# Encoder layer on one core: the look-ahead for each row's largest score takes 64 rows a product, two products side by side, and stands in twos

## The chip, the core and the metric

One core of a Trainium2 chip. The time is the device time of one execution in microseconds; the kernel before takes 1884.24 us, the median of three runs (1882.11 to 1884.48). The engines are TensorE (PE; PEld for its weight loads), VectorE (DVE), ScalarE (ACT), GpSimd (POOL) and the DMA queue of SyncE (SP).

## The reference

One layer of an encoder runs on two sequences with shared weights, "prompt" of 1,024 and "sample" of 2,048 tokens, width 1,024, in float32. Cut to what matters:

```python
h = rms_norm(x, norm_pre)
u_pool, g_pool, q, k, v, g_attn, q_x, g_x = jnp.split(jnp.einsum('btd,de->bte', h, w_in), SPLITS, axis=-1)
pool_out = multiscale_pool(u_pool, pool_w, pool_scale) * jax.nn.silu(g_pool)
# 8 query heads, 2 key/value heads, 64 wide
q = apply_rope(rms_norm(q, q_norm), cos, sin)
k = apply_rope(rms_norm(k, k_norm), cos, sin)
s = jnp.einsum('bqkgd,bskd->bkgqs', qblk, k) * 64 ** -0.5
p = jax.nn.softmax(s, axis=-1)
attn_out = jnp.einsum('bkgqs,bskd->bqkgd', p, v) * jax.nn.silu(g_attn)
# 4 heads over 256 memory tokens
x_out = memory_attention(q_x, k_m, v_m) * jax.nn.silu(g_x)
y = jnp.einsum('bte,ed->btd', jnp.concatenate([pool_out, attn_out, x_out], -1), w_out)
return x + rms_norm(y, norm_post)
```

A softmax needs a shift near the largest score of its row, so that the exponentials neither overflow nor vanish; any shift near it gives the same result.

## The kernel before, in words

**Two stages.** The first (up to some 700 us) normalises, projects and stores queries, keys, values, gates and the pool in DRAM scratch. Most products are made of three: each operand is split into a high part that the PE's fast float32 form (F32R) holds exactly and a low part, and high x high, high x low and low x high are added. The second stage, from some 700 us on, is the attention and the output, and the change lies there.

**Groups.** The second stage works on pairs of 128-token blocks, eight pairs of the sample and then four of the prompt. A pair has three groups (class `Group`): kinds 0 and 1 are the self-attention with key head 0 and 1 (256 queries x 4 heads, in two halves j of 512 columns), kind 2 the attention over the memory. A group walks its keys in chunks of 128: 16 in the sample, 8 in the prompt, 2 for the memory. One chunk of one group is a **slot**, so a sample pair has 34 slots, a prompt pair 18, and all have 344.

**Score operands.** Scores are computed transposed, keys on the partitions. KA holds the keys' high part in rows 0 to 63 and the low part in rows 64 to 127; qa holds the queries' high part twice. One product KA x qa so gives high x high plus low x high. KB holds the high part again in rows 0 to 63 and ones in row 64; qb holds the queries' low part and, in row 64, minus the largest score: the second product, of 65 rows, adds high x low and the shift.

**A slot.** The loop over the slots emits, in this order: `weights(k, 0)` (two products into one of the two PSUM buffers S, line 220, then the exponential on ACT into P, line 227); `sums` of the chunk before (P added up in z, on DVE, lines 239 and 240, half on POOL in the sample); loads; a look, if the plan has one here; things due; `weights(k, 1)`; pieces of an earlier pair's output projection (`Output.piece`, lines 359 to 361), spread over the slots between two points; things due at the half. Every fourth slot's half brings the value products of four chunks (`values`, line 252): float32 products with weights 64 columns wide, whose two j go to the two halves of the array side by side. Their slot is the first of a run of four, k%4 = 0. Order on PE, ACT, DVE and POOL is that of the program (`manual_schedule`); SP's is the scheduler's.

**Looks.** `largest` (lines 177 to 196) computes the shift ahead of the group: for 128 queries against 1,024 keys it makes two 512-wide products qa x KA into a PSUM tile N (two banks; the pool psn has two such buffers), line 191, for kind 2 four of 256 columns, line 183, and a negated maximum on DVE, line 194. So the largest is that of (high + low keys) x high queries. The last look of a group calls `shift` (line 198): the two halves' minima, a 32 x 32 transpose, and DMAs that put the row into qb's row 64. `shift` also loads KB, if this sequence's part isn't there, and the low queries. A group has 16 looks in the sample, 8 in the prompt, 2 for the memory: 344 in all, 320 of two products and 24 of four.

**The plan of looks** runs backwards over the slots, one look a slot, each for the nearest later group that starts more than LEAD = 4 slots on. 20 looks come before slot 0: they stand among the last projection's products, one after each second term (`look_ahead`). A group's loads come three slots before its first look.

**A group's end.** With n the next group's first slot: at n + 1.5 the column totals of z (`totals`, line 260, products of 32 columns) go into a tile N; at n + 2 `take` multiplies the values by the gate; at n + 2.5 `inverse` takes the reciprocal of the totals on DVE (line 272), which ends the use of that N, and sends it round through DRAM to be multiplied in (`mix_out`). A buffer of psn goes to whatever next asks while it is free; there is no fixed turn.

Of the kernel before, what the change touches and what calls it, by code (L numbers as in the profile page):

```python
# [7 lines left out]
F32 = mybir.dt.float32  # L8
F32R = mybir.dt.float32r
# [14 lines left out]
def encoder(ctx, tc, I, O):  # L24


    nc = tc.nc
# [44 lines left out]
    KA, KB, V = [], [], []  # L72

    def open_early():
        for kind in range(2):
            KA.append(early.tile([128, 2048], F32R, name=f"KA{kind}"))
            KB.append(early.tile([128, 2048], F32R, name=f"KB{kind}") if kind == 0 else None)
        KA.append(early.tile([128, 2, 2, NMEM], F32R, name="KA2"))
        KB.append(early.tile([128, 2, 2, NMEM], F32R, name="KB2"))
        for t in KB[0], KB[2]:  # L80
            nc.vector.memset(t[64:65].bitcast(F32), 1.0)

        for name in ("top",):
            lanes32[name] = [early.tile([128, 32], F32, name=f"{name}{n}") for n in range(2)]
            for t in lanes32[name]:
                nc.vector.memset(t, 0.0)
# [3 lines left out]
    def load_K(s, kind, t, hl, h):  # L90
        if (s, kind, t is KA, hl) in has_K:
            return
        has_K.add((s, kind, t is KA, hl))
        if kind == 2:
            src = DKM[hl, :, :, s].rearrange("d (c j) m -> d c j m", j=2)
            nc.sync.dma_start(out=t[2][h:h + 64].bitcast(F32), in_=src)
            return
        for a in range(0, SEQS[s][1], 1024):
            nc.sync.dma_start(out=t[kind][h:h + 64, a:a + 1024].bitcast(F32), in_=DK[s][kind][hl, :, a:a + 1024])
# [25 lines left out]
    def lanes_to_rows(t, name):  # L125

        r = early.tile([128, 32], F32, name="rows32", tag=f"r{name}", bufs=2)
        nc.vector.transpose(out=r, in_=t)
        return r
# [3 lines left out]
    class Group:  # L133
# [11 lines left out]

        def load(self):
            s, p, kind = self.s, self.p, self.kind
            for hl in range(2):
                load_K(s, kind, KA, hl, 64 * hl)
            self.qa = early.tile([128, 2, 512], F32R, name="qa", tag="qa", bufs=4)  # L150
            for h in range(2):
                self.load_q(self.qa[64 * h:64 * h + 64], 0)
            self.top = lanes32["top"][self.n % 2]
            if self.parts > 1:
                self.nb = early.tile([128, self.parts, 8], F32, name="nb", tag="nb", bufs=2)
# [20 lines left out]

        def largest(self, n):
            a, lane = self.pieces[n]
            S = psn.tile([128, 1024], F32, name="N", tag="N")
            if self.kind == 2:  # L180
                j = lane
                for x in range(4):
                    nc.tensor.matmul(S[:, 256 * x:256 * x + 256],
                                     lhsT=self.qa[:, j, 128 * x:128 * x + 128],
                                     rhs=KA[2][:, x // 2, j], start=True, stop=True)
                out, S = self.top[:, 4 * j:4 * j + 4], S.rearrange("p (x k) -> p x k", x=4)
            else:
                q = self.qa[:, lane // 4, 128 * (lane % 4):128 * (lane % 4) + 128]
                for b in range(2):
                    k = 1024 * a + 512 * b  # L190
                    nc.tensor.matmul(S[:, 512 * b:512 * b + 512], lhsT=q,  # L191
                                     rhs=KA[self.kind][:, k:k + 512], start=True, stop=True)
                out = self.nb[:, a, lane:lane + 1] if self.parts > 1 else self.top[:, lane:lane + 1]
            nc.vector.tensor_reduce(out=out, in_=S, axis=AX.X, op=ALU.max, negate=True)  # L194
            if n == len(self.pieces) - 1:
                self.shift()

        def shift(self):

            if self.parts > 1:  # L200
                nc.vector.tensor_tensor(out=self.top[:, 0:8], in0=self.nb[:, 0], in1=self.nb[:, 1],
                                        op=ALU.min)
            self.qb = early.tile([128, 2, 512], F32R, name="qb", tag="qb", bufs=3)
            load_K(self.s, self.kind, KB, 0, 0)
            self.load_q(self.qb[0:64], 1)
            r = lanes_to_rows(self.top, "top")
            row = self.qb[64:65].rearrange("o j (l b r) -> o (j l) b r", b=4, r=32)
            for b in range(4):
                nc.sync.dma_start(out=row[:, :, b].bitcast(F32), in_=r[32 * b:32 * b + 8])


        def weights(self, k, j):
            if j == 0:
                self.P[k] = dbl.tile([128, 2, 512], F32, name="P", tag="P", bufs=6)
            S = pss.tile([128, 512], F32, name="S", tag="S")
            keys = slice(128 * k, 128 * k + 128)
            for n, (K, q) in enumerate(((KA, self.qa[:, j]), (KB, self.qb[0:65, j]))):
                rows_ = slice(0, 128 if n == 0 else 65)
                if self.kind < 2:
                    nc.tensor.matmul(S, lhsT=K[self.kind][rows_, keys], rhs=q, start=n == 0, stop=n == 1)  # L220
                    continue
# [178 lines left out]
    LEAD, RUN = 4, 4  # L400
    pairs = [Pair(s, p) for s in (1, 0) for p in range(SEQS[s][1] // 256)]
    groups = []
# [5 lines left out]
    slots = [(g, k) for g in groups for k in range(g.chunks)]  # L408
# [3 lines left out]
    def at(slot, f, *args):  # L412

        later.setdefault(slot, []).append((f, args))

    def due(slot):
        for f, args in later.pop(slot, ()):
            f(*args)  # L418

    first = {}  # L420
# [18 lines left out]
    for g in groups:  # L439
        n, c = first[g], g.chunks  # L440
# [11 lines left out]

    looks, n = {}, len(slots)
    left = {g: list(range(len(g.pieces))) for g in groups}
    while any(left.values()):
        n -= 1
        able = [g for g in groups if left[g] and first[g] - LEAD > n]
        if able:  # L460
            looks[n] = (able[0], left[able[0]].pop())
    ahead = [looks[n] for n in sorted(looks) if n < 0]
    loads = {}
    for n, (g, k) in looks.items():
        if k == 0:
            loads.setdefault(max(n - 3, -1), []).append(g)

    order = {mybir.EngineType.PE, mybir.EngineType.Activation, mybir.EngineType.DVE,
             mybir.EngineType.Pool}

    def look_ahead():

        if ahead:
            g, n = ahead.pop(0)
            g.largest(n)


    with ExitStack() as p1:
# [345 lines left out]
        early = psn = None  # L824
        for sb, (kind, s, nb, b0) in enumerate(SB):
            groups = groups_of(sb)
            nxt = []
            for gi, (src, pieces, run) in enumerate(groups):
# [7 lines left out]
                if last and gi == 3:  # L836
                    front.close()
                    early = ctx.enter_context(tc.tile_pool(name="early", bufs=1, side="right", reuse_waits="tile"))
# [22 lines left out]
    own = pool("p2one", 1)  # L861
# [4 lines left out]

    ones = own.tile([128, 32], F32, name="ones")
    nc.vector.memset(ones, 1.0)
    KB[1] = own.tile([128, 2048], F32R, name="KB1")
    nc.vector.memset(KB[1][64:65].bitcast(F32), 1.0)  # L870
    V += [own.tile([128, 16, 64], F32, name=f"V{kind}") for kind in range(2)]
    V.append(own.tile([128, 2, 4, 64], F32, name="V2"))
    wo_hi = own.tile([128, NC, D], F32R, name="wo_hi")
# [3 lines left out]
    with tc.manual_schedule(engines=order):  # L877
        slot = 0
        while slot < len(slots) or later or fill:
            g, k = slots[slot] if slot < len(slots) else (None, 0)  # L880
            if g:
                g.weights(k, 0)
            if 0 < slot <= len(slots):
                h, kh = slots[slot - 1]
                h.sums(kh)
            for x in loads.get(slot, ()):
                x.load()
            if slot in looks:
                looks[slot][0].largest(looks[slot][1])
            due(slot)  # L890
            if g:
                g.weights(k, 1)
            pauses = sum(x is None for x in fill)
            n = -(-(len(fill) - pauses) // max(1, until[0] - slot - pauses)) if fill else 0
            for _ in range(n):
                x = fill.pop(0)
                if x is None:
                    break
                out, h, c, start, final = x
                out.piece(h, c, start, final)  # L900
                if final:
                    if h == 0 and not out.last:

                        for n in sorted(later):
                            for x in [x for x in later[n] if x[0].__name__ in ("square", "norm", "out")]:
                                later[n].remove(x)
                                x[0](*x[1])
                    at(slot + END, out.half_out, h)
                    at(slot + 1 + END, out.square, h)
                    if h == 1:  # L910
                        at(slot + 2, out.norm)
                        at(slot + 3, out.out)
            due(slot + END)
            slot += 1

# [41 lines left out]
```

## Time and profile before

| | |
|---|---|
| median of three runs | 1884.24 us |
| span of the profiled execution | 1878.7 us |
| first S product, last slot's first product | 699.1 us, 1836.6 us |
| eight sample pairs, three prompt pairs | 850.6 us, 216.8 us |
| mean granted clock of TensorE | 0.994 |

The three runs are all the times there are; the profiled execution's own is its span, first to last instruction, and the median lies 5.6 us above it.

How to read the lines: "L191 PE MATMUL N<-KA,qa 128*128 128x512 f32 x640 | 207.5, 405 | 17.9 <-..." is a group: line, engine, operation, tiles written and read, weight and data shape, count; busy us of the group as a union, mean ns of one; idle time of the engine before them and what ended it. PE's records overlap, since a product begins while the last is still leaving the array: what a product costs is the distance to the next one's start. A time line has start, length, engine and the same names, and merges neighbours of one kind ("x16"); a value product in float32 leaves two records, so four chunks make 16. A window has its length, then for PE, PEld, DVE, ACT and POOL the busy time and count, then the granted clock, the DMA share and GB/s.

### The profile page before, as it was taken

The numbers are of one execution on the slowest core, as the hardware profiler recorded it, in microseconds if no ns is written. First come the engines' busy times: TensorE is split into PE (matmuls) and PEld (weight loads), VectorE is DVE, ScalarE is ACT, GpSimd is POOL, SyncE is SP. The second block draws the span as 40 slices with busy tenths as digits, with TensorE's granted clock in tenths as the row PEclk, the third lists the DMA queues.
The fourth block names the chain that finished last, engine by engine and source line by source line (L and its number), as shares of the span: only waits on it lengthen the run. The fifth ranks groups of instructions, "written<-read, shape, count | busy, mean of one in ns | idle before, by whom it ended". The sixth has DMA issues, their size and how long they took to land. (4 is left out here: it accounts for less than half of the span.)

```text
span 1878.7 us, 23531 instructions
## 1 busy us (share of the span) xinstructions
PE 1813.4 (97%) x8520; PEld 1279.4 (68%) x8520; DVE 1135.6 (60%) x1312; ACT 696.8 (37%) x1266; POOL 846.5 (45%) x748
## 2 busy tenths in 40 slices
PE   7999999999999999999999999999999999999997
PEld 6888888988988884465564656556465655565564
DVE  7745145431544168867768576776858576757744
ACT  5523234222422115444435344443434343333331
POOL 3655016520446007845638374563837452413311
PEclk9999999999999999999999999999999999999998
DMA  7634454254434926212122221212222153223211
GB/s 244 201 113 120 108 162 132 73 154 116 121 99 114 216 65 173 73 27 79 48 79 62 68 62 29 80 45 79 63 68 63 51 137 78 96 85 96 87 43 62
DMA packets 148485, 181.83 MB, mean 97 GB/s; under 512 B 21504, under 2 KB 118416, under 8 KB 148368
## 3 DMA queue, kind: packets, MB, share of 16 engines
q1 hardware_dynamic: 148368, 180.33, 33.9%
q8 instruction: 67, 1.10, 0.3%
q14 instruction: 50, 0.41, 0.1%
HBM read 126.50 MB, written 53.62 MB: 96 GB/s over the span
## 5 line engine op out<-in xcount | busy, mean ns | idle before, releaser
L227 ACT ACTIVATE P<-S 128x512 f32<-128x512 f32 x688 | 399.3, 598 | 555.5 <-PE S L220 430.8
L194 DVE TENSOR_REDUCE nb<-N 128x1 f32<-128x1024 f32 x256 | 311.7, 1218 | 239.8 <-PE N L191 239.0
L239 POOL TENSOR_TENSOR z<-z,P 128x512 f32<-128x512 f32 x224 | 318.4, 1421 | 222.5 <-ACT P L227 217.4
L252 PE MATMUL acc<-P,V 128*64 128x512 f32 (+1 forms) x1472 | 319.4, 576 | 0.5
L220 PE MATMUL S<-qa,KA 128*128 128x512 f32 x640 | 274.6, 429 | 9.7 <-ACT P L227 9.7
L63 POOL TENSOR_TENSOR rs<-rs,mhalf 128x1 f32<-128x1 f32 (+2 forms) x100 | 101.0, 1013 | 401.8 <-DVE rs L61 401.8
L240 DVE TENSOR_TENSOR z<-z,P 128x512 f32<-128x512 f32 (+1 forms) x272 | 271.0, 996 | 13.1 <-ACT P L227 12.9
L220 PE MATMUL S<-qb,KB 65*128 65x512 f32 x640 | 254.0, 397 | 0.0
L550 PE MATMUL pz<-hT_hi,w_hi 128*128 128x512 f32 x592 | 233.1, 394 | 1.3 <-ACT vmst L808 0.8
L552 PE MATMUL pz<-hT_hi,w_lo 128*128 128x512 f32 x592 | 232.1, 392 | 0.5 <-DVE w_lo L69 0.5
L551 PE MATMUL pz<-hT_lo,w_hi 128*128 128x512 f32 x592 | 232.3, 392 | 0.0
L191 PE MATMUL N<-KA,qa 128*128 128x512 f32 x640 | 207.5, 405 | 17.9 <-DVE rz L272 11.2
L252 PEld LDWEIGHTS acc<-P,V 128*64 128x64 f32 x1472 | 98.3, 138 | 178.7 <-issue 169.6
L220 PEld LDWEIGHTS S<-qa,KA 128*128 128x128 f32 x640 | 120.4, 188 | 143.9 <-issue 72.6
L194 DVE TENSOR_REDUCE top<-N 128x1 f32<-128x1024 f32 (+1 forms) x88 | 107.0, 1219 | 94.3 <-PE N L191 74.5
L191 PEld LDWEIGHTS N<-KA,qa 128*128 128x128 f32 x640 | 116.6, 191 | 60.9 <-DVE nb L194 21.9
L550 PE MATMUL pz<-w_hi,hT_hi 128*128 128x384 f32 (+1 forms) x416 | 140.2, 338 | 0.9 <-ACT hT_hi L68 0.8
L551 PE MATMUL pz<-w_lo,hT_hi 128*128 128x384 f32 (+1 forms) x416 | 139.4, 335 | 0.8 <-DVE w_lo L69 0.8
L552 PE MATMUL pz<-w_hi,hT_lo 128*128 128x384 f32 (+1 forms) x416 | 139.7, 338 | 0.0
L359 PE MATMUL py<-wo_hi,mix 128*128 128x512 f32 x352 | 137.7, 391 | 0.0
L360 PE MATMUL py<-wo_lo,mix 128*128 128x512 f32 x352 | 137.7, 391 | 0.0
L361 PE MATMUL py<-wo_hi,mix 128*128 128x512 f32 x352 | 137.4, 390 | 0.0
(120 smaller groups left out, 2479.5 us busy)
## 6 DMA issues: line engine op xcount, KB each, us to landing
wraw<-w_in SPq DMA_DIRECT2D x15, 1536.0 KB
dg<-gst SPq DMA_DIRECT2D x48, 256.0 KB
qa<-dq SPq DMA_DIRECT2D x48, 256.0 KB
gz<-rows SPq DMA_DIRECT2D x72, 128.0 KB
x<-x_sample SPq DMA_DIRECT2D x16, 512.0 KB
xr<-x_sample SPq DMA_DIRECT2D x16, 512.0 KB
y_sample<-xr SPq DMA_DIRECT2D x16, 512.0 KB
dq<-qst SPq DMA_DIRECT2D x96, 64.0 KB
```

The costliest lines, as they stand in the source:

```text
L191: nc.tensor.matmul(S[:, 512 * b:512 * b + 512], lhsT=q, rhs=KA[self.kind][:, k:k + 512], start=True, stop=True)
L194: nc.vector.tensor_reduce(out=out, in_=S, axis=AX.X, op=ALU.max, negate=True)
L220: nc.tensor.matmul(S, lhsT=K[self.kind][rows_, keys], rhs=q, start=n == 0, stop=n == 1)
L227: nc.scalar.activation(out=self.P[k][:, j], in_=S, func=AF.Exp)
L239: nc.gpsimd.tensor_tensor(out=z[:, :cut], in0=a[:, :cut], in1=P[:, :cut], op=ALU.add)
L240: nc.vector.tensor_tensor(out=z[:, cut:], in0=a[:, cut:], in1=P[:, cut:], op=ALU.add)
L252: nc.tensor.matmul(self.acc[64 * j:64 * j + 64, x], lhsT=v, rhs=P[:, j, x], start=(k, i) == (0, 0), stop=k == self.chunks - 1, skip_group_ ...
L359: nc.tensor.matmul(ps, lhsT=mh, rhs=wo_hi[:, c, cols], start=first, stop=False)
L360: nc.tensor.matmul(ps, lhsT=mh, rhs=wo_lo[:, c, cols], start=False, stop=False)
L550: nc.tensor.matmul(ps, lhsT=sh, rhs=mh, start=c == 0, stop=False)
L551: nc.tensor.matmul(ps, lhsT=sh, rhs=ml, start=False, stop=False)
L552: nc.tensor.matmul(ps, lhsT=sl, rhs=mh, start=False, stop=c == n - 1)
```

## The change

- The looks take KA and KB in halves: KA's rows 64 to 127 now hold the keys' high part and its rows 0 to 63 the low part (for the scores nothing changes, since qa holds the high queries twice), and KB's rows 0 to 63 hold the high part as before. Each product of a look takes 64 rows: the one over rows 0 to 63 reads KB, the one over rows 64 to 127 KA. They write different banks. For kind 2 the four products go in the order 0, 2, 1, 3, so that neighbours take different halves and banks.
- A look is so high x high alone; the low part of the keys no longer enters the largest score.
- The plan gives two looks to slots with k%4 = 0 and k%4 = 2, none to the others (before slot 0 one each, as before). In slots with k%4 = 2 they stand where the look stood, ahead of `weights(k, 1)`; in slots with k%4 = 0 they stand behind the output pieces, right before the value products. A group's last look so comes 6 slots ahead of it instead of 5.
- KB is loaded with KA, ahead of the first look, instead of in `shift`; KB1 moves from the second stage's pool to the one that is opened early, with its memset.

```diff
@@ def open_early
-            KB.append(early.tile([128, 2048], F32R, name=f"KB{kind}") if kind == 0 else None)
+            KB.append(early.tile([128, 2048], F32R, name=f"KB{kind}"))
...
-        for t in KB[0], KB[2]:
+        for t in KB:
             nc.vector.memset(t[64:65].bitcast(F32), 1.0)
@@ Group.load
+            load_K(s, kind, KB, 0, 0)
             for hl in range(2):
-                load_K(s, kind, KA, hl, 64 * hl)
+                load_K(s, kind, KA, hl, 64 - 64 * hl)
@@ Group.largest
+            halves = (slice(0, 64), KB), (slice(64, 128), KA)
             S = psn.tile([128, 1024], F32, name="N", tag="N")
             if self.kind == 2:
                 j = lane
-                for x in range(4):
+                for x in (0, 2, 1, 3):
+                    rows_, K = halves[x // 2]
                     nc.tensor.matmul(S[:, 256 * x:256 * x + 256],
-                                     lhsT=self.qa[:, j, 128 * x:128 * x + 128],
-                                     rhs=KA[2][:, x // 2, j], start=True, stop=True)
+                                     lhsT=self.qa[rows_, j, 128 * x:128 * x + 128],
+                                     rhs=K[2][rows_, x // 2, j], start=True, stop=True)
...
                 for b in range(2):
                     k = 1024 * a + 512 * b
-                    nc.tensor.matmul(S[:, 512 * b:512 * b + 512], lhsT=q,
-                                     rhs=KA[self.kind][:, k:k + 512], start=True, stop=True)
+                    rows_, K = halves[b]
+                    nc.tensor.matmul(S[:, 512 * b:512 * b + 512], lhsT=q[rows_],
+                                     rhs=K[self.kind][rows_, k:k + 512], start=True, stop=True)
@@ Group.shift
-            load_K(self.s, self.kind, KB, 0, 0)
@@ the plan of looks
+    def room(n):
+        return 1 if n < 0 else (2, 0, 2, 0)[slots[n][1] % 4]
...
-        able = [g for g in groups if left[g] and first[g] - LEAD > n]
-        if able:
-            looks[n] = (able[0], left[able[0]].pop())
+        for _ in range(room(n)):
+            able = [g for g in groups if left[g] and first[g] - LEAD > n]
+            if able:
+                looks.setdefault(n, []).insert(0, (able[0], left[able[0]].pop()))
...
+    def look(slot):
+        for g, n in looks.pop(slot, ()):
+            g.largest(n)
@@ the loop over the slots
-            if slot in looks:
-                looks[slot][0].largest(looks[slot][1])
+            if k % 4:
+                look(slot)
             due(slot)
...
+            look(slot)
             due(slot + END)
```

More of the change, by code (lines that the diff above doesn't have):

```diff
@@ L458, in encoder @@
         n -= 1
-        able = [g for g in groups if left[g] and first[g] - LEAD > n]
-        if able:
-            looks[n] = (able[0], left[able[0]].pop())
-    ahead = [looks[n] for n in sorted(looks) if n < 0]
+        for _ in range(room(n)):
+            able = [g for g in groups if left[g] and first[g] - LEAD > n]
+            if able:
+                looks.setdefault(n, []).insert(0, (able[0], left[able[0]].pop()))
+    ahead = [x for n in sorted(looks) if n < 0 for x in looks[n]]
     loads = {}
-    for n, (g, k) in looks.items():
-        if k == 0:
-            loads.setdefault(max(n - 3, -1), []).append(g)
+    for n in looks:
+        for g, k in looks[n]:
+            if k == 0:
+                loads.setdefault(max(n - 3, -1), []).append(g)
     order = {mybir.EngineType.PE, mybir.EngineType.Activation, mybir.EngineType.DVE,
              mybir.EngineType.Pool}
+    def look(slot):
+        for g, n in looks.pop(slot, ()):
+            g.largest(n)
     def look_ahead():
@@ L868, in encoder @@
     nc.vector.memset(ones, 1.0)
-    KB[1] = own.tile([128, 2048], F32R, name="KB1")
-    nc.vector.memset(KB[1][64:65].bitcast(F32), 1.0)
     V += [own.tile([128, 16, 64], F32, name=f"V{kind}") for kind in range(2)]
```

## The prediction

> **What bounds the kernel now.** I read the page's head first.
>
> ```profile
> span 1878.7 us, 23531 instructions
> ...
> PE 1813.4 (97%) x8520; PEld 1279.4 (68%) x8520; DVE 1135.6 (60%) x1312; ACT 696.8 (37%) x1266; POOL 846.5 (45%) x748
> ```
>
> TensorE looks like the bound, and the change halves one of its groups. But busy PE time is a union of overlapping, modelled durations, so the next views are the time line of PE, for what a product costs and where PE waits, and the window view of one pair, which puts prices on stages. The first of these groups is the exponential, the other three belong to a look:
>
> ```profile
> L227 ACT ACTIVATE P<-S 128x512 f32<-128x512 f32 x688 | 399.3, 598 | 555.5 <-PE S L220 430.8 <-issue 72.9 <-POOL o L290 25.0
> ...
> L194 DVE TENSOR_REDUCE nb<-N 128x1 f32<-128x1024 f32 x256 | 311.7, 1218 | 239.8 <-PE N L191 239.0
> ...
> L191 PE MATMUL N<-KA,qa 128*128 128x512 f32 x640 | 207.5, 405 | 17.9 <-DVE rz L272 11.2 <-DVE nb L194 5.7
> ...
> L183 PE MATMUL N<-KA,qa 128*128 128x256 f32 x96 | 16.0, 288 | 2.1 <-DVE top L194 2.1
> ```
>
> A look is two 512-wide products (320 of them) or four 256-wide ones (24), then a maximum of 1.22 us on DVE. The time line gives the step of a product and the price of changing the array's shape:
>
> ```profile
> 999.44 0.39 PE L220 MATMUL S<-qb,KB 65*128 65x512 f32 x1
> 999.76 3.65 PE L252 MATMUL acc<-P,V 128*64 128x512 f32 x16
> 1003.34 0.50 PE L220 MATMUL S<-qa,KA 128*128 128x512 f32 x1
> 1003.68 0.39 PE L220 MATMUL S<-qb,KB 65*128 65x512 f32 x1
> 1003.91 0.63 PE L191 MATMUL N<-KA,qa 128*128 128x512 f32 x2
> 1004.38 0.39 PE L220 MATMUL S<-qa,KA 128*128 128x512 f32 x1
> ```
>
> A full product follows the last after 0.23 us, a look takes 0.47 (1003.91 to 1004.38). Into the value products (64 columns each, two at a time) the step is 0.32, so entering costs 0.09; the eight pairs at 0.43 account for 3.43 of the 3.58 us up to 1003.34, the other 0.15 being a late second pair and the way out; the next full product also comes after 0.34 instead of 0.23. In all a stay in the other shape costs about 0.14 on the way in and 0.20 on the way out, 0.34 us.
>
> The rows on which the argument turns come next: two slots without a look and without output pieces, and two with one look each.
>
> ```profile
> 1790.00 0.41 PE L220 MATMUL S<-qa,KA 128*128 128x512 f32 x1
> ...
> 1790.85 0.50 PE L220 MATMUL S<-qa,KA 128*128 128x512 f32 x1 [0.21 <-ACT P L227]
> 1791.19 0.39 PE L220 MATMUL S<-qb,KB 65*128 65x512 f32 x1
> 1791.42 0.42 PE L220 MATMUL S<-qa,KA 128*128 128x512 f32 x1
> ...
> 1792.84 0.36 PE L224 MATMUL S<-qa,KA 128*128 128x256 f32 x1
> ```
> ```profile
> 1790.20 1.08 ACT L227 ACTIVATE P<-S 128x512 f32<-128x512 f32 x2 [0.34 <-PE S L220]
> 1791.62 1.14 ACT L227 ACTIVATE P<-S 128x512 f32<-128x512 f32 x2 [0.34 <-PE S L220]
> ```
> ```profile
> 1546.81 0.42 PE L220 MATMUL S<-qa,KA 128*128 128x512 f32 x1
> ...
> 1547.30 0.63 PE L191 MATMUL N<-KA,qa 128*128 128x512 f32 x2
> ...
> 1548.22 0.48 PE L220 MATMUL S<-qa,KA 128*128 128x512 f32 x1
> ```
>
> Without a look a slot lasts 1.42 us (1790.00 to 1791.42, 1791.42 to 1792.84), with one 1.41. Two S buffers make a ring: products 0.34 and 0.23, 0.04 to the exponential, 0.55 to 0.60 for it, 0.05 back. The ring, not PE, sets a slot that has no pieces, and one look stands in its gap for nothing. About half of the slots are of this kind.
>
> **The change, part by part.** *Products.* Of the 344 looks (320 + 24) 20 come before slot 0 and 324 in slots; counted through the plan's loop, these make 87 twos beside the value products (k%4 = 0) and 75 in the third slot (k%4 = 2). If two half-height products run side by side, as the two half-width ones above do, a look takes 0.235: 324 x 0.235 = 76 us less PE work. That is gross, and here is what stands against it.
>
> *Shape changes.* No row shows a 64-row product. The nearest is the value products' stay, 0.34 us in and out. Bounds for a third-slot two: 0 (the array need not empty for a change of rows) to twice the 0.34, since a weight load of 128 columns would stand open there. Beside the values only one more change is added, so half of each. I take 0.34 and 0.14: the one change of shape in the trace always costs. 75 x 0.34 + 87 x 0.14 = 38 us. The Trainium skill (TensorEngine Tiling, Key Properties) has the rule against this change: a new tiling mode, though not a new tile in the same mode, drains TensorE. By that rule the 38 stay and the sum is 1921; without it they go, and it is the first rival's 1881. That page counts row tiling among the modes; here only column tiling shows it. The skill also has four-row packing at 3.07 times instead of four (TensorE: Matmul & The Clock Gate, Measured speedup vs the span model); an estimate from that share, 0.31 a look for 0.235, would add up to 23 us gross.
>
> *Stages.* One sample pair, cut at its runs of four slots (fifth: the memory group's two):
>
> ```profile
> 1117.42:1128.54 11.12, 10.74 (x50) 5.34 (x49) 8.50 (x10) 4.68 (x8) 9.56 (x8) 1.00 0.39 102
> 1128.54:1138.95 10.41, 9.81 (x42) 5.07 (x40) 8.41 (x9) 4.83 (x9) 6.01 (x5) 1.00 0.17 52
> 1138.95:1154.00 15.05, 15.05 (x70) 10.21 (x70) 10.20 (x13) 5.54 (x10) 9.07 (x7) 1.00 0.00 0
> 1154.00:1168.82 14.82, 14.82 (x66) 9.87 (x64) 7.48 (x10) 5.81 (x11) 3.88 (x3) 1.00 0.01 2
> 1168.82:1178.95 10.13, 10.13 (x58) 5.93 (x57) 5.57 (x8) 3.38 (x7) 1.84 (x2) 1.00 0.41 103
> 1178.95:1192.49 13.54, 13.09 (x71) 8.94 (x68) 10.08 (x11) 5.88 (x11) 7.88 (x5) 1.00 0.61 175
> 1192.49:1206.01 13.52, 13.52 (x60) 8.78 (x59) 8.72 (x10) 4.68 (x8) 4.46 (x4) 1.00 0.07 23
> 1206.01:1216.59 10.58, 10.04 (x42) 5.16 (x42) 8.04 (x10) 6.39 (x13) 9.08 (x7) 1.00 0.09 25
> 1216.59:1226.59 10.00, 9.93 (x42) 5.21 (x42) 9.93 (x11) 4.53 (x8) 9.92 (x7) 1.00 0.29 103
> sum 109.17, PE 107.12 PEld 64.51 DVE 76.93 ACT 45.72 POOL 61.71; mean PE 11.90 PEld 7.17 DVE 8.55 ACT 5.08 POOL 6.86
> ```
>
> *A run without pieces* (second, eighth, ninth), walked in the new order with the ring's numbers, 0 being its second slot's first product. That slot takes 1.43. In the third, the first S product ends at 2.0, the two looks run from 2.09 to 2.61, the second S product starts at 2.70. The fourth starts at 3.27, but its second product waits for the exponential of 2.70's S until 4.13. The next first slot starts at 4.70, its second product again waits, until 5.56; looks 6.22 to 6.74, values 6.88 to 10.31, and the run ends at 10.4. Measured before: 10.41, 10.58, 10.00. So nothing is gained: second and fourth slot lose a look that was free, third and first get two that are not. I take 0, +0.2 and +0.4 (one of 10.58's slots also holds pieces).
>
> *A run with pieces* is PE's own (13.52 of 13.52): 4 x 0.235 less, 0.34 and 0.14 more, -0.46. Fourth and seventh run: -0.5 each; third, whose first slot has no pieces, and fifth: 0.
>
> *A group's end* gets worse. Its total takes one of the two N buffers in the second slot and gives it back at the reciprocal, which DVE has behind the third slot's maxima. Before:
>
> ```profile
> 1236.65 0.73 PE L191 MATMUL N<-KA,qa 128*128 128x512 f32 x2 [0.31 <-DVE nb L194]
> ...
> 1238.91 0.50 PE L191 MATMUL N<-KA,qa 128*128 128x512 f32 x1 [0.59 <-DVE rz L272]
> ```
> ```profile
> 1235.37 1.23 DVE L194 TENSOR_REDUCE nb<-N 128x1 f32<-128x1024 f32 x1
> 1236.51 0.68 DVE L266 TENSOR_TENSOR o<-acc,gate 128x512 f32<-128x512 f32 x1
> 1237.11 1.75 DVE L272 RECIPROCAL rz<-N 128x256 f32<-128x256 f32 x1
> ```
>
> The look at 1236.65 waits for the maximum before it (1235.37 + 1.23), since the total holds the other buffer. With two looks in that slot the second can only take the first one's buffer: after its product (0.4) and its maximum (1.22) it starts 1.7 us after the first instead of 0.24, about 1.45 us of PE at 31 of the 36 group ends (after the other five no look is left), and the S product, ACT and all of PE queue behind it. What before paid there (as above) goes. Walked like the run above, the first run, 11.12, becomes 12.4 (+1.3); the sixth holds two ends, 13.54 becomes 15.8 (+2.3).
>
> A pair: 1.3 + 0 + 0 - 0.5 + 0 + 2.3 - 0.5 + 0.2 + 0.4 = +3.2, eight pairs +26.
>
> *Sequence of 1,024.* The stage of the first three pairs:
>
> ```profile
> 1549.70:1766.48 216.78, 206.74 (x962) 130.34 (x961) 147.62 (x144) 80.03 (x153) 59.79 (x34) 0.99 0.30 87
> ```
>
> 72.3 a pair, with three group ends in 18 slots and pieces in few of them: the same terms give +3.5 for the ends, -0.5 and -0.3 for pieces and rest, +2.7; three pairs and the few looks of the last, +9.
>
> *The rest.* The 20 early looks stand alone among full products: 0.235 + 0.34 for 0.47, +2 us. KB's loads (256 KB each, six for kinds 0 and 1) move on SP's queue from after a group's looks to ahead of its KA and queries; they are issued three slots (over 4 us) before the first look, or some 30 us before it in the projections, so I put them at 0, and at a transfer of some 2 us for each of three later kinds if that cover fails. KB1's memset goes from one side of the stage to the other: 0. DVE's maxima are as many and as long. The loss of the low part changes only the shift.
>
> Sum: 26 + 9 + 2 = +37 us on the profiled execution's 1878.7, so 1916; the median of the runs lies 5.6 over that span (1884.24 - 1878.67), which gives 1921.
>
> **Rivals.** *Rows change shape free.* Then the 38 and the 2 fall away and the sum is -3: 1881. For it: only column shapes are seen to cost. It shows in the step from the last S product to a look, 0.23 instead of 0.32.
>
> *The second look at a group's end finds a buffer.* -31 x 1.2 = -37: 1884. Against it is the row at 1236.65.
>
> *PE's saving comes out whole* (faster): PE is the bound in every slot, so 76 less and 40 more count in full, -36: 1848. It decides if slots without a look fall below 1.42 us; the slots at 1790 speak against it, 97% PE for it.
>
> *The halves run one after the other.* A look stays at 0.47 and the changes of shape are added: some 60 of the 76 us come back (the rest is in the ring's gaps): 1981. Against it the value products, two records to each step.
>
> **How the numbers follow.** Forecast 0.60, free rows 0.14, buffer found 0.06, whole saving 0.10, halves in turn 0.10. A measurement of this kernel tells apart 0.2%, 4 us. Slower: all of halves in turn, 0.58 of the forecast, 0.06 of the two rivals near zero: 0.74. Same: 0.08 from these. Faster: whole saving and the rest, 0.18. Range 1870 to 1962: the upper end is the forecast with the shape changes at twice their price (+38) and a little over, the lower one the free rows with a wait of 1.1 instead of 1.45 us at the 31 ends (-11); left out are the last two rivals, 0.2.
>
> **What would show it.** Right: look products of one pair start within 0.02 us; the step into a two is about 0.32 and the S product after it 0.09 late; slots without pieces or look stay at 1.4; in 31 places the second look starts 1.5 us or more after the first, released by DVE; PE waits on ACT grow, DVE busy time is unchanged. Wrong: if the first and the sixth run of the pair above do not grow, or if runs without pieces fall below 9.7 us.

## The result, and the profile after

The changed kernel takes 1986.71 us (median of 4 runs, 1985.69 to 1989.26) where the kernel before takes 1883.17 (4 runs, 1878.91 to 1884.48): ratio 1.0557, 95% interval 1.0541 to 1.0572. It is slower, as forecast, but by 104 us instead of 37, and 25 us above the upper end of the range. In the profiled executions the span grows by 107 us, from 1878.7 to 1985.8.

The head of the changed kernel's page, the lines that answer to those shown of before:

```profile
span 1985.8 us, 23531 instructions
...
PE 1868.0 (94%) x8520; PEld 1224.0 (62%) x8520; DVE 1219.5 (61%) x1312; ACT 684.0 (34%) x1266; POOL 836.3 (42%) x748
...
PEclk9999999999999988999998999989998999899999
```

PE is busy for 55 us longer although its looks were halved, and the clock row has eights in the second stage, which begins in the fifteenth slice. Before, that row had only nines up to its last slice:

```profile
PEclk9999999999999999999999999999999999999998
```

The slices round, so the trace's clock records were added up: TensorE spends 155.1 us at half of its clock (23 stretches, the last at the very end of the trace) where it spent 25.4 before (5 stretches). The cores view agrees: a mean clock of 0.961 over 1985.8 us is 2 x 0.039 x 1985.8 = 155 us at a half.

The windows of the two stages (length; busy time and count of PE, PEld, DVE, ACT, POOL; clock; DMA share; GB/s), the sample's eight pairs and the prompt's three, first before (the sample alone; the prompt's row stands in the prediction), then after:

```profile
699.11:1549.70 850.59, 828.38 (x3701) 493.52 (x3700) 610.43 (x638) 368.28 (x668) 497.51 (x341) 1.00 0.26 72
```
```profile
700.70:1633.40 932.70, 868.60 (x3702) 450.96 (x3700) 683.42 (x636) 356.51 (x668) 493.76 (x342) 0.94 0.23 65
1633.40:1871.90 238.50, 216.97 (x962) 122.78 (x961) 156.48 (x143) 78.55 (x153) 55.05 (x34) 0.94 0.27 78
```

So of the 107 us the sample has 82.1 (forecast 26), the prompt's three pairs 21.7 (9), what comes before slot 0 has 1.6 (2), and the rest 1.7. PE's busy time in the sample grows by 40 us, but the stage by 82: the other 42 are waits.

The same pair as in the prediction, cut at the same slots:

```profile
1162.25:1175.88 13.63, 11.62 (x50) 4.98 (x49) 11.65 (x11) 4.64 (x8) 8.06 (x7) 0.93 0.25 58
1175.88:1188.28 12.40, 11.90 (x42) 4.92 (x41) 8.29 (x9) 4.70 (x9) 7.11 (x5) 0.80 0.14 44
1188.28:1203.41 15.13, 14.85 (x69) 9.25 (x69) 11.82 (x12) 5.36 (x10) 8.00 (x6) 1.00 0.00 0
1203.41:1218.36 14.95, 14.69 (x66) 8.77 (x64) 8.69 (x10) 5.65 (x12) 4.29 (x4) 1.00 0.01 2
1218.36:1228.26 9.90, 9.90 (x56) 5.53 (x56) 6.39 (x8) 3.10 (x7) 5.02 (x4) 1.00 0.37 98
1228.26:1245.82 17.56, 14.69 (x71) 9.31 (x68) 11.83 (x11) 5.65 (x11) 4.73 (x4) 0.90 0.44 140
1245.82:1259.39 13.57, 13.33 (x59) 7.73 (x57) 7.71 (x8) 4.50 (x9) 3.86 (x3) 1.00 0.07 21
1259.39:1269.85 10.46, 9.70 (x40) 4.29 (x41) 9.95 (x9) 6.12 (x13) 8.92 (x7) 1.00 0.09 26
1269.85:1280.83 10.98, 10.13 (x42) 4.26 (x41) 10.70 (x11) 4.47 (x8) 10.82 (x8) 1.00 0.34 121
sum 118.58, PE 110.80 PEld 59.03 DVE 87.04 ACT 44.19 POOL 60.81; mean PE 12.31 PEld 6.56 DVE 9.67 ACT 4.91 POOL 6.76
```

The three runs of four that grew most, the first, the second and the sixth, are the three with a clock below 1.00. They are where a group ends, and right behind. The time line of PE there (start, length; in brackets the idle time before it and what ended it):

```profile
1170.83 0.50 PE L195 MATMUL N<-KB,qa 64*128 64x512 f32 x1
1170.83 0.50 PE L195 MATMUL N<-KA,qa 64*128 64x512 f32 x1
...
1172.98 0.49 PE L195 MATMUL N<-KB,qa 64*128 64x512 f32 x1 [1.65 <-DVE nb L198]
1172.98 0.49 PE L195 MATMUL N<-KA,qa 64*128 64x512 f32 x1
1173.40 0.50 PE L223 MATMUL S<-qa,KA 128*128 128x512 f32 x1
1173.74 0.43 PE L223 MATMUL S<-qb,KB 65*128 65x512 f32 x1
1173.98 0.62 PE L223 MATMUL S<-qa,KA 128*128 128x512 f32 x1
1174.39 0.63 PE L223 MATMUL S<-qb,KB 65*128 65x512 f32 x1
1174.86 0.79 PE L223 MATMUL S<-qa,KA 128*128 128x512 f32 x1
1175.45 0.63 PE L223 MATMUL S<-qb,KB 65*128 65x512 f32 x1
...
1179.06 4.49 PE L255 MATMUL acc<-P,V 128*64 128x512 f32 x16
```

The wait of the forecast is there: the second look starts 2.15 us after the first, released by DVE's maximum. What the forecast did not have comes behind it. From 1173.98 on the S products last 0.62 to 0.79 us instead of 0.39 to 0.50, and follow each other at 0.41 to 0.59 instead of 0.23 and 0.34. The value products at 1179.06 take 4.49 us; before they took 3.65. That is the half clock, and here it lasts 6.8 us.

Setting the clock records beside all 31 group ends with two looks shows how regular this is. PE waits 1.65 to 1.67 us at ten of them, and behind each of the ten the clock falls. At fifteen it waits 1.32 or 1.33 us, and the clock falls behind three. The remaining six waits, from 1.45 to 3.65 us, have four falls in or behind them. That makes 17 of the stage's 22 falls; the other five, of 3.4 us each, stand elsewhere and have no wait of this kind.

Beside values and in third slots the halves do run side by side. The time line of PE in a third slot:

```profile
1185.30 0.39 PE L223 MATMUL S<-qb,KB 65*128 65x512 f32 x1
1185.62 0.49 PE L195 MATMUL N<-KB,qa 64*128 64x512 f32 x1
1185.63 0.49 PE L195 MATMUL N<-KA,qa 64*128 64x512 f32 x1
1185.96 0.39 PE L195 MATMUL N<-KB,qa 64*128 64x512 f32 x1
1185.96 0.39 PE L195 MATMUL N<-KA,qa 64*128 64x512 f32 x1
1186.28 0.50 PE L223 MATMUL S<-qa,KA 128*128 128x512 f32 x1
1186.62 0.40 PE L223 MATMUL S<-qb,KB 65*128 65x512 f32 x1
```

The two products of a look start within 0.01 us. The way in takes 0.32 instead of 0.23 (1185.30 to 1185.62), the first pair 0.34, the second, with the way out, 0.32, and the next full product 0.34 more. Six steps of full products would be 1.38 us from 1185.30 to 1186.62; it is 1.32.

### The profile page after: what moved, and what is told of

Same layout as the page of the kernel before. It is cut to its first block, busy times and chain, and to the rows that moved or that the text cites. A ratio compares the mean times of both kernels' runs of the same rounds, so it can differ in the third digit from the quotient of the medians.

```text
span 1985.8 us, 23531 instructions
## 1 busy us (share of the span) xinstructions
PE 1868.0 (94%) x8520; PEld 1224.0 (62%) x8520; DVE 1219.5 (61%) x1312; ACT 684.0 (34%) x1266; POOL 836.3 (42%) x748
## 5 line engine op out<-in xcount | busy, mean ns | idle before, releaser
L230 ACT ACTIVATE P<-S 128x512 f32<-128x512 f32 x688 | 387.1, 598 | 673.5 <-PE S L223 445.5
L243 DVE TENSOR_TENSOR z<-z,P 128x512 f32<-128x512 f32 (+1 forms) x272 | 326.7, 1201 | 146.6 <-ACT P L230 140.7
L198 DVE TENSOR_REDUCE nb<-N 128x1 f32<-128x1024 f32 x256 | 303.3, 1216 | 122.5 <-PE N L195 122.2
L255 PE MATMUL acc<-P,V 128*64 128x512 f32 (+1 forms) x1472 | 341.3, 609 | 0.0
L223 PE MATMUL S<-qa,KA 128*128 128x512 f32 x640 | 305.7, 478 | 34.9 <-ACT P L230 34.7
L223 PE MATMUL S<-qb,KB 65*128 65x512 f32 x640 | 267.4, 418 | 0.0
L223 PEld LDWEIGHTS S<-qa,KA 128*128 128x128 f32 x640 | 126.1, 197 | 222.4 <-ACT P L230 121.7
L255 PEld LDWEIGHTS acc<-P,V 128*64 128x64 f32 x1472 | 103.5, 146 | 197.7 <-issue 190.7
L195 PE MATMUL N<-KB,qa 64*128 64x512 f32 x320 | 137.6, 487 | 44.0 <-DVE nb L198 35.6
L195 PE MATMUL N<-KA,qa 64*128 64x512 f32 x320 | 137.6, 487 | 0.0
```

Source lines behind the costliest of these rows:

```text
L195: nc.tensor.matmul(S[:, 512 * b:512 * b + 512], lhsT=q[rows_], rhs=K[self.kind][rows_, k:k + 512], start=True, stop=True)
L230: nc.scalar.activation(out=self.P[k][:, j], in_=S, func=AF.Exp)
L243: nc.vector.tensor_tensor(out=z[:, cut:], in0=a[:, cut:], in1=P[:, cut:], op=ALU.add)
L255: nc.tensor.matmul(self.acc[64 * j:64 * j + 64, x], lhsT=v, rhs=P[:, j, x], start=(k, i) == (0, 0), stop=k == self.chunks - 1, skip_group_ ...
```

## The experiments

The theory after the result: the group ends' wait, by itself priced nearly right, makes the clock fall to a half, and the slow products behind it are most of what is missing. The rivals: the half-height products cost more than 0.34 a stay; twos of any height cost it, by the ring and the waits; the moved loads cost something. In each diff below the lines stand against the changed kernel, unless another is named; "..." marks what is left out. "Half-clock time" is added up from the clock records of the profiled execution.

**Work in the wait.** Six spare full-height products at each group's end, between the two looks. They go into the S buffer that the next S product overwrites, so the result stays as it is:

```diff
+        here = looks.pop(slot, ())
+        for i, (g, n) in enumerate(here):
+            if i and slot in ends:
+                keep_busy(slots[slot][0], 6)
+            g.largest(n)
```

> The changed kernel with six dummy full-height products between the two looks at each of the 31 group ends (into an S buffer that the next S product overwrites; results unchanged). Theory, clock: 155 us of the changed kernel's profile run at half the clock (25 before), set off by PE standing idle while the second look waits; of its +107 us of span about 65 are that lost clock. Then added work makes it faster: low-clock time under 70 us, time about 1945 us (1930 to 1960). Rival, waits alone: where the clock is low PE waits for others anyway, so it costs nothing; 1987 us within 5, or slower.

Measured: 1942.93 us, ratio 1.0319 (1.0295 to 1.0343). Added work makes the changed kernel 44 us faster. Its page:

```profile
span 1940.1 us, 23903 instructions
...
PEclk9999999999999999999999999999999999999998
```

The half-clock time falls from 155.1 to 18.8 us. ACT's hold on S, on the other hand, stays as it was in the changed kernel; the view of waits (us in all, times, longest), first after, then with the spare products:

```profile
PEld S L223 <- ACT P L230: 121.7, 225, 1.7
```
```profile
PEld S L232 <- ACT P L239: 123.0, 226, 1.7
```

So it is the clock and not the ring that the added work mends. Its half-clock time is no more than that of the kernel before (25.4 us).

**Work where PE is idle for other reasons.** Two spare products in odd slots in which no piece is pending:

```diff
+            if g and k % 2 and not fill:
+                keep_busy(g, 2)
             if k % 4:
                 look(slot)
```

> The changed kernel with two dummy full-height products in every slot with odd k that holds no output pieces, where a look of the kernel before stood (results unchanged). If the exp ring sets these slots, the products cost nothing there. Theory, clock, in the form that a stretch of about 3.4 us with PE working under half of it halves the next one: more work in the look-free slots shortens the low stretches but does not take away the idle time that sets them off: low-clock time 155 to about 90 to 120 us, time 1960 to 1975 us. Rival, waits alone: 1987 us or up to 15 slower.

Measured: 1983.84 us, 1.0540 (1.0514 to 1.0567), half-clock time 127.8, outside the 90 to 120 and the 1960 to 1975 us that were expected, and at the rival's 1987 within 5. But the edit did much less than its expectation says. Its condition asks for an empty list of pieces, and from the second sample pair on that list also holds the pauses between pieces. The view of the spare products' line (count, duration in ns, first and last start) shows where they stand:

```profile
L139 PE MATMUL S<-qa,KA x42: 390/397/796, 705.7 to 827.3; 128*128 128x512 f32 x42
```

So there are 42 of them, in 21 slots: the 17 odd slots of the first sample pair and four of the second. From slot 0 to slot 34 the half-clock time fell from 27.3 to 6.8 us and the pair from 105.7 to 100.3 us; the pairs from the third on have no spare product. This run so does not say what such work is worth behind the waits of the other pairs, nor whether it is free in the ring's gap. As far as it goes, it agrees with the clock theory.

**Seven products of half height in the wait**, which need no change of shape against the looks beside them. Here the lines stand against the first experiment's kernel:

```diff
-                             lhsT=KA[g.kind][:, 0:128] ..., rhs=g.qa[:, 0], ...)
+                             lhsT=KB[g.kind][0:64, 0:128] ..., rhs=g.qa[0:64, 0], ...)
-                keep_busy(slots[slot][0], 6)
+                keep_busy(slots[slot][0], 7)
```

> As the run with the six dummies at the group ends, but with seven of half height in the looks' own shape, one after the other. They add the same busy time and no change of shape. If the clock follows the time in which PE works, whatever the height: low-clock time under 40 us and 31 times 0.34 us less than that run, about 1932 us. If it follows how much of the array works: low-clock time near 100 us, 1955 to 1975 us.

Measured: 1940.19 us, 1.0302 (1.0272 to 1.0333), half-clock time 34.2; the time lies 8 us above what was expected, the half-clock time inside it. Products that use half of the array hold the clock up about as well as full ones, so the clock goes by the time in which PE works rather than by the share of the array that does. This pair, whole, has no half clock in it and so shows what the change costs without:

```profile
1146.86:1160.01 13.15, 12.53 (x56) 5.79 (x56) 11.17 (x11) 4.55 (x8) 8.07 (x6) 1.00 0.26 60
...
1185.66:1200.64 14.98, 14.72 (x66) 8.78 (x64) 8.70 (x10) 5.66 (x12) 4.30 (x4) 1.00 0.00 0
...
1210.54:1226.57 16.03, 15.81 (x85) 10.61 (x81) 10.42 (x9) 5.55 (x11) 4.24 (x4) 1.00 0.48 145
1226.57:1240.14 13.57, 13.33 (x60) 7.72 (x58) 9.14 (x10) 4.52 (x9) 4.68 (x4) 1.00 0.13 33
...
1250.61:1261.58 10.97, 10.13 (x41) 4.26 (x41) 10.69 (x11) 4.48 (x8) 10.81 (x8) 1.00 0.33 121
...
1146.86:1261.58 114.72, 110.81 (x502) 60.47 (x502) 86.78 (x83) 43.99 (x84) 61.46 (x44) 1.00 0.20 58
```

These are the first, fourth, sixth, seventh and ninth run and the whole pair: 114.72 us, where before has 109.17 and the change 118.58.

**One look at a group's end, the other in the next slot:**

```diff
+    ends = {first[g] + g.chunks + 2 for g in groups}
...
+        if n in ends or n - 1 in ends:
+            return 1
         return 1 if n < 0 else (2, 0, 2, 0)[slots[n][1] % 4]
```

> The changed kernel's plan with one look instead of two in the slot where a group's total holds an N buffer, and one in the slot after it. Both theories say that the wait of about 1.5 us at 31 ends goes, some 40 us; the clock theory adds most of 65 us of lost clock: 1885 to 1905 us, low-clock time under 50 us. Waits alone: 1945 us.

Measured: 1929.65 us, 1.0244 (1.0223 to 1.0265), half-clock time 55.4; a pair without half clock takes 111.90 us. It is the best of the versions that keep the twos elsewhere, but 25 us above what was expected at most, and the half-clock time is over 50: the ends do not carry all that is left. Of that pair's 2.7 us over the kernel before, 1.3 lie in the second run (11.74 for 10.41) and 1.0 in the ninth (10.97 for 10.00).

**Only the height, only the twos, only the loads.** One look a slot as before, but of two half-height products:

```diff
-        return 1 if n < 0 else (2, 0, 2, 0)[slots[n][1] % 4]
+        return 1 if n < 0 else 1
...
-            if k % 4:
-                look(slot)
+            look(slot)
```

> Half-height products side by side, but one look a slot where the look stood before: the product form without the twos. By the terms of the forecast each look saves 0.235 us and pays 0.34 us for two changes of shape, +34 us if PE set every slot, some +20 with the gaps of the exp ring; no wait at group ends is added. So 1900 to 1915 us and low-clock time under 60 us. Rival (shape changes free): 1870 us or less.

Measured: 1913.61 us, 1.0156 (1.0134 to 1.0178), half-clock time 46.1, as expected. Run seven, which is PE's own, goes from 13.52 to 14.14:

```profile
1210.46:1224.60 14.14, 14.14 (x59) 7.82 (x58) 9.66 (x10) 4.67 (x8) 4.11 (x5) 1.00 0.08 22
```

Each of its four slots takes 0.15 to 0.17 us more: a stay costs 0.235 + 0.155 = 0.39, and one look saves only 0.235.

The twos of the plan, but each look over all 128 rows of KA:

```diff
-                for x in (0, 2, 1, 3):
-                    rows_, K = halves[x // 2]
+                for x in range(4):
+                    rows_, K = slice(0, 128), KA
...
-                    rows_, K = halves[b]
+                    rows_, K = slice(0, 128), KA
```

> The twos alone: the changed plan with the full-height products of before (no change of shape, nothing side by side). If the twos (waits at group ends, look-free slots bound by the exp ring) are the cost and the half-height products a gain in PE time: without lost clock some 36 us above the changed kernel's 1922 (1987 less 65 of clock), and with the array working longer per slot less clock lost than 65, so 1960 to 1990 us and low-clock time 60 to 120 us. Rival, the changes of shape are the main cost: 1925 us or less.

Measured: 1983.68 us, 1.0534 (1.0501 to 1.0566), half-clock time 98.1. This too is as expected: the twos alone cost as much as the whole change, and on top of them half height changes the total by nothing. By slots it does gain: in the seventh run of the pair shown, the slot with the values takes 6.66 us instead of 6.92 and the third 3.16 instead of 3.21. But the changed kernel has 57 us more at half clock, 155.1 against 98.1; that this is what eats the gain was not tried.

Both edits together, so that nothing is left but the moved loads and buffers:

> Only the change's moved loads and buffers (KB with KA, the high part in KA's rows 64 to 127, KB1 in the early pool), with the products and the plan of before. Every theory has these at nothing: 1884 us within 4. If it is over 1890, part of the +103 is theirs.

Measured: 1882.02 us, 1.0002 (0.9989 to 1.0016). The loads cost nothing.

**Both halves on rows 0 to 63**, where two products cannot run at one time:

```diff
-            halves = (slice(0, 64), KB), (slice(64, 128), KA)
+            halves = (slice(0, 64), KB), (slice(0, 64), KB)
```

> The changed kernel with both halves of a look on rows 0 to 63, so that they cannot run side by side (same values). If they do run side by side in the changed kernel, 344 times 0.235 us come on top, of which some 60 us show outside the ring's gaps, less some clock, since the array works longer: 2005 to 2040 us. If they did not gain from it: 1987 us within 5.

Measured: 2083.77 us, 1.1063 (1.1030 to 1.1095). Running side by side is worth 97 us to the changed kernel, more than the 18 to 53 expected, and the half-clock time was to shrink and grew, to 222.6 us. The prediction's gross saving of 76 us and 67 us more at half clock, at the first experiment's rate of 44 us for 136, would make 76 + 22 = 98; but why the clock falls more often here was not settled.

**The sums behind the looks.** DVE's addition of z stands ahead of the maxima. In slots with a two in third place it is emitted behind them:

```diff
+            two = k % 4 == 2 and slot in looks
-            if 0 < slot <= len(slots):
+            if 0 < slot <= len(slots) and not two:
...
             if k % 4:
                 look(slot)
+            if two:
+                slots[slot - 1][0].sums(slots[slot - 1][1])
```

> The changed kernel, only that in the slots with k%4 = 2 which hold two looks the column sums z of the chunk before (half on DVE, half on POOL in the sample) are emitted behind the two looks instead of ahead of them, so that both maxima stand before the addition on DVE. If DVE's addition, which takes 1.4 us there and stands ahead of the first maximum, is what made the second look at a group's end start 2.15 us after the first instead of the 1.7 us of the forecast, it now starts 1.65 to 1.75 us after it, 31 x 0.45 = 14 us come back, and a part of the half-clock time with them (155 us now): 1945 to 1975 us. If DVE's place in the order is not the cause (the first look itself is late, or the maxima run one after the other anyway and only they count), the step stays above 2 us and the time at 1980 to 1990. If the later sums hold the P buffers and so ACT, the waits of ACT on DVE and POOL grow and it is slower than 1990.

Measured: 1976.36 us, 1.0500 (1.0476 to 1.0524), half-clock time 122.9. DVE's place in the order is a cause, but a small one. The end shown above now has the second look 1.82 us behind the first; the time lines of PE and of DVE:

```profile
1167.21 0.50 PE L195 MATMUL N<-KA,qa 64*128 64x512 f32 x1
...
1169.03 0.49 PE L195 MATMUL N<-KB,qa 64*128 64x512 f32 x1 [1.32 <-DVE nb L198]
```
```profile
1167.75 1.23 DVE L198 TENSOR_REDUCE nb<-N 128x1 f32<-128x1024 f32 x1 [1.78 <-PE N L195]
```

Counted over the 31 ends, only ten had 2.15 to 2.17 in the changed kernel, and fifteen had 1.82 or 1.83 already; one, behind an addition of 2.37 us, had 4.15. The mean goes from 2.03 to 1.83, 6 us in all and not the 14 expected. The 32 us less at half clock would by the first experiment's rate (44 us for 136) be worth 10 by themselves, so the two do not add up cleanly. Nor does the length of a wait alone decide on the clock: here PE waits 1.32 or 1.33 us at every end, and the clock falls behind 13 of the 31, where in the changed kernel it fell behind 3 of 15 such waits.

**A better plan.** One full-height look a slot as before, and half-height twos only beside values where the next slot has pieces, so that both look places are really PE's. The form of a look and its place in the loop follow from the set `twos`. First at three places of a sample pair and one of a prompt pair:

```diff
+    twos = {first[pair.groups[0]] + r for pair in pairs[1:] for r in ((12, 16, 22) if pair.s else (8,))}
...
-        return 1 if n < 0 else (2, 0, 2, 0)[slots[n][1] % 4]
+        return 2 if n in twos else 0 if n - 1 in twos else 1
```

> One full-height look a slot as before, but beside the value products whose next slot holds output pieces (three places in each sample pair after the first, one in each prompt pair) two half-height looks side by side, and none in that next slot. In the changed kernel these places alone gained: the slot of the value products grew by 0.21 to 0.23 us, the next one fell by 0.45 to 0.47. So 25 places times 0.25 us, 6 us: 1877 us against 1883, ratio 0.9966, low-clock time as before (under 35 us). If half-height looks lose wherever they stand: 1885 us or more.

Measured: 1885.44 us, 1.0012 (1.0001 to 1.0023); a gain was expected. The fourth and the seventh run gained, 14.82 to 14.62 and 13.52 to 13.22, but the memory group's run rose from 10.13 to 10.25 and the prompt's places, which the plan had taken for PE's own, by 1 to 5 us each. The same plan at full height:

> The same plan with full-height looks throughout: it moves a look of 0.47 us from one slot that PE sets to another, so 1883 us within 3. If the plan and not the form brings the gain: 1877 us too.

Measured: 1887.89 us, 1.0032 (1.0023 to 1.0042), slower than expected: the plan by itself costs some 6 us. At the same places half height is then worth 2.4 us. With the two places that gained, and no others (against the first of these two kernels):

```diff
-    twos = {first[pair.groups[0]] + r for pair in pairs[1:] for r in ((12, 16, 22) if pair.s else (8,))}
+    twos = {first[pair.groups[0]] + r for pair in pairs[1:] for r in ((12, 22) if pair.s else ())}
```

> The plan of the run before it, cut to the places whose runs fell there: the fourth and the seventh run of each sample pair (13.52 to 13.22 and 14.83 to 14.62 us in that trace), without the memory group's place (10.13 to 10.25) and the prompt's (12.96 to 14.07). Seven or eight pairs times 0.5 us: -4 us, 1878 against 1882, ratio 0.998. If the time stays at 1882, what the runs gained is given back elsewhere.

Measured: 1878.96 us, 0.9981 (0.9970 to 0.9993), the only version that beats the kernel before, and by 3.4 us. Its fourth and seventh run, both PE's own for their whole length:

```profile
1153.45:1168.07 14.62, 14.62 (x66) 9.33 (x64) 7.71 (x10) 5.60 (x11) 3.87 (x3) 1.00 0.01 2
...
1191.64:1204.86 13.22, 13.22 (x59) 8.30 (x58) 10.03 (x10) 4.47 (x8) 3.87 (x3) 1.00 0.07 23
```

## Why the prediction was wrong, step by step

**What failed above all: the clock was left out.** The prediction took each product at its full-clock step and let "the S product, ACT and all of PE queue behind" the wait, without asking what the wait does to PE itself. Every row of its pair had a clock of 1.00 and the prompt's 0.99, and it took that to stay so. Each of the ten waits of 1.65 us and over at a group's end was followed by a fall of the clock to a half, for 6.8 or 10.2 us, and shorter ones were so at times. Holding it up gave 44 us back, shown by the first experiment. With no more half-clock time than before the change takes 1940 to 1943 us, inside the range.

The rest lies in terms of the sum. The pair without half clock is 114.72 - 109.17 = 5.6 us longer, not 3.2.

**A run with pieces, -0.46 each: measured about 0.** The seventh run took 13.57 for 13.52, the fourth 14.98 for 14.82 (forecast 13.0 and 14.3). In the seventh run, by the distances of the slots' first products on the time line of PE, its four slots changed from 6.45, 2.89, 2.78 and 1.40 us to 6.66, 2.42, 3.16 and 1.34: +0.21 beside the values, -0.47, +0.38 in the third slot, -0.06. The forecast has +0.14, -0.47, +0.34 and -0.47. The step that failed most is the last: it took such a run to be PE's in all four slots, but the fourth holds no pieces, so what its look took was free already, in the ring's gap.

**The group's end, +1.3 in the first run and +2.3 in the sixth: measured +2.0 and +2.5** (13.15 for 11.12, 16.03 for 13.54). The second look starts 2.03 us after the first, the mean of the 31 ends, instead of 1.7. The rows of the experiment with the sums behind the looks show what it takes without DVE's addition in front: 0.54 from the first product to the maximum where the forecast took 0.4, 1.23 for it and 0.05 back. At ten ends 0.33 for DVE's addition came on top.

**DVE "busy time is unchanged": it grew.** The maxima are as many and as long as forecast; the addition of z is not. Its group, first before, then after:

```profile
L240 DVE TENSOR_TENSOR z<-z,P 128x512 f32<-128x512 f32 x224 | 205.8, 919 | 3.1 <-ACT P L227 3.0
```
```profile
L243 DVE TENSOR_TENSOR z<-z,P 128x512 f32<-128x512 f32 x224 | 257.3, 1149 | 114.4 <-ACT P L230 109.2
```

Before, a look's maximum mostly kept DVE from the addition while POOL did its half: 167 of the 224 came directly behind a maximum. After the change 72 do, and in the other slots both halves are released by the same exponential. So 113 of the 224 additions take 1.4 us or more, where 29 did before; all 113 start while POOL is at work. The time lines of DVE and of POOL in the changed kernel:

```profile
1181.03 0.68 DVE L243 TENSOR_TENSOR z<-z,P 128x512 f32<-128x512 f32 x1
...
1185.43 1.46 DVE L243 TENSOR_TENSOR z<-z,P 128x512 f32<-128x512 f32 x1 [3.72 <-ACT P L230]
```
```profile
1185.05 1.29 POOL L242 TENSOR_TENSOR z<-z,P 128x512 f32<-128x512 f32 x1 [1.39 <-ACT P L230]
```

Alone the addition takes 0.68 us; beside POOL's it takes 1.46 and ends 0.55 us after POOL's does (1186.89 against 1186.34). The Trainium skill has this (SBUF — State Buffer, Who interferes with whom): an instruction of VectorE with two inputs in SBUF contends with one of GpSimd that reads SBUF, for ports that it calls an exclusive lock. The rows agree: of the 0.68 us that the addition takes alone, 0.55 fall behind POOL's end. What it is worth was tried in the third slots alone: 10 us, with the clock's part in them.

**The ninth run, +0.4: measured +1.0** (10.97 for 10.00). Whether that is DVE's longer addition or the walk of the ring was not tried apart.

The terms nearly close: 37 us of the forecast and 8 x (5.6 - 3.2) = 19 for these steps make 56, where the kernel with the seven products in its waits lies 1940.19 - 1880.39 = 60 above the kernel before in its own comparison. By stages its eight sample pairs are 46.8 us longer (26 + 19 = 45) and the prompt's three 12.5 (forecast 9).

**What was right.** The halves run side by side (the rival of halves in turn is 97 us worse when tried). Shape changes cost at a change of rows as at one of columns, 0.09 on the way in, so the rival of free rows falls, and the rule of the Trainium skill that the prediction weighed (TensorEngine Tiling, Key Properties) agrees with the rows: 0.34 forecast, 0.38 (the third slot above) and 0.39 measured for a two and for a single look. The second look at an end finds no buffer, so that rival falls too. PE's saving did not come out whole, since slots without look and pieces stay at 1.34 to 1.47 us. PE's waits on ACT grew, from 53.4 us to the 121.7 shown; before:

```profile
PEld S L220 <- ACT P L227: 53.4, 170, 1.2
```

The early looks cost +1.6 us, and up to 3.9 in the experiments that leave them as they are here (forecast 2); the loads cost nothing, as forecast. Of the runs without pieces the second and the eighth went about as walked: 10.54 and 10.47 without half clock, where the walk ends at 10.4. The +0.2 added to the eighth's 10.58 did not come.

## What to carry to other kernels

Before work is taken from TensorE or put together, look at what is left in the stretches where it will wait: a wait of under 2 us can halve the clock for several, and spare products in that wait can be a gain. A saving per product counts only in slots that the engine fills itself, so price each slot by its own limit (here a ring of two buffers that hides one look for nothing). A pack of half-height products pays only where it saves more than its 0.38 to 0.39 us of shape changes, or shares a change that is made anyway (beside the values it was 0.21).

## What the runs showed of the hardware

The clock changed only between full and half, in stretches of multiples of 3.41 us (but for the last, which the end of the trace cuts). Full products of 512 columns follow each other at 0.43 us at half clock, so 0.213 us of PE work can be counted for each 512 columns at full. By that estimate the 3.41 us ahead of a fall held a share of work of 0.27 to 0.51 in the changed kernel (the fall at the end of the trace aside); the lowest share without a fall behind it was 0.41. The two overlap, so the runs give no exact threshold. The Trainium skill (TensorE: Matmul & The Clock Gate, Part 1: The HAM clock gate) tells of the same window and the same two states, but its table lets the clock fall after an idle window; here a window with a wait of 1.65 us, or at times of 1.32, and products in the rest was enough.
